# A hybrid decoder block on one core: input of the feed-forward part made earlier, weights prepared in pieces

## The chip, the cores and the metric

The kernel runs on 1 of the 8 cores of one Trainium2 chip. The metric is device time in microseconds (us) of one execution. TensorE (PE in the profile) multiplies matrices, VectorE (DVE), ScalarE (ACT) and GpSimd (POOL) work on elements, SyncE (SP) issues every DMA of this kernel in order.

## The reference

One decoder layer, `x` of 2048 tokens by 1024 channels, float32:

```
h = RMSNorm(x);  P = h @ W_in            # split among three mixers and three gates
ya, yb, yc = RG-LRU, mLSTM, stick-breaking attention (each projected to 1024)
x = x + (sigmoid(g_a)*ya + sigmoid(g_b)*yb + sigmoid(g_c)*yc) @ W_o
hf = RMSNorm(x);  gate, up = split(hf @ W_ffn_in)      # 2 x 2816 columns
x = x + (silu(gate)*up) @ W_ffn_out
out = RMSNorm(x)
```

## The kernel before

Tokens are worked in 4 chunks of 512 (c = 0 to 3), channels in tiles of 128 partitions. The stages follow each other: S (projections, LRU, mLSTM, attention), then `G` and `G_out` for each chunk, then F1 (feed-forward in), then F2 (feed-forward out and the last norm). The code is written with a tile library: a scheduler orders the instructions of each engine by the program's order as priority and by its own estimate of when an operand is there; tiles come from pools, and a tile waits until the memory it takes is free. What stands in an engine's queue then runs strictly in that order.

`G` computes the gates and merges the branches (tiles `pg`, `py`, `mh`, `ml`); `G_out` multiplies by W_o (`po`), adds x, writes x1 to `dX1` and sums its squares. At its end `rstd` makes the norm's factors: a product with ones (`pss`), a power on GpSimd (`nrs`), diagonals (`ndg`), a product that spreads them over the partitions (`psr`).

The feed-forward part uses Strassen-Winograd products: blocks of two by two, seven products instead of eight, each in three f16 products (high and low part). A weight block is loaded (`raw`), summed on GpSimd (`sm`, lines 826 to 829), scaled by an exponent (`squares` on ScalarE, `pse` on TensorE, `power` on VectorE) and split into `wh` (ScalarE) and `wl` (VectorE) by `wforms`. `F_input` does the same for the normed input of two chunks: four loads, four norms on VectorE (line 904), four sums on GpSimd (848 to 851), high parts on ScalarE (908), low parts on VectorE (909); it yields 4 tiles `f` (k = 0 to 3) of 7 forms. Chunks 0 and 1 form one side (cp = 0), chunks 2 and 3 the other (cp = 1).

F1 runs 22 weight blocks for each side, 84 products a block: 3696 products. `forms` splits the result of each pair of blocks and writes it to `dA`; F2 reads it back in three groups of pairs (0 to 3, 4 to 7, 8 to 10), 1848 products. `F2_scales` takes the largest exponent over all 11 pairs before the first weight of F2 can be scaled.

Of the kernel before, what the change touches and what calls it, by code (L numbers as in the profile page):

```python
# [18 lines left out]
P = 128  # L19
# [16 lines left out]
class Trunk:  # L36
# [10 lines left out]
    def setup(self):  # L47
# [20 lines left out]
        self.dR2 = dr.tile([NCH, P, CH], F32, name="dR2")  # L68
        self.dRow = dr.tile([NCH, 2, 4, CH], F32, name="dRow")
        self.dA = dr.tile([2, NPAIR, P, 7, 2, CH], F16, name="dA")  # L70
        self.dX2 = dr.tile([KT, 2, P, CH], F32, name="dX2")

# [4 lines left out]
    def constants(self):  # L77
        nc, cp = self.nc, self.cp

        def const(name, shape):  # L80
            t = cp.tile(shape, F32, name=name)
            nc.sync.dma_start(t, self.I[name])
            return t

        self.g2 = const("g_ffn", [P, KT])
        self.g3 = const("g_fin", [P, KT])
# [8 lines left out]
        for nm in ("wa", "wx"):  # L95
            for j in range(2):
                t = cp.tile([P, P], F32, name=f"bd{nm}{j}")
# [56 lines left out]
    HO = None  # L154

# [56 lines left out]
    def rstd(self, pool, acc, tag, bufs, ps="m", copy=True, sqrt=False, ps0=None):  # L212

        nc, V = self.nc, self.nc.vector
        ps0 = ps0 or ps
        pss = self.ps.tile([P, CH], F32, tag=ps0, name="pss", bufs=self.NP[ps0])
# [4 lines left out]
        rs = self.rs = pool.tile([P, NB], F32, tag="nrs", name="nrs", bufs=2)  # L221
        if sqrt:
            nc.scalar.activation(rs, pss[:, :NB], AF.Sqrt, scale=1.0 / 1024.0, bias=self.eps)
            V.reciprocal(rs, rs)
        else:
            V.tensor_scalar(rs, pss[:, :NB], 1.0 / 1024.0, 1e-6, op0=ALU.mult, op1=ALU.add)
            nc.gpsimd.tensor_tensor(rs, rs, self.nhalf, op=ALU.pow)
        dg = pool.tile([P, NB, P], F32, tag=tag, name="ndg", bufs=bufs)
        for b in range(NB):
            V.tensor_scalar(dg[:, b, :], self.idn, rs[:, b : b + 1], None, op0=ALU.mult)  # L230
        psr = self.ps.tile([P, CH], F32, tag=ps, name="psr", bufs=self.NP[ps])
        for b in range(NB):
            nc.tensor.matmul(psr[:, b * P : (b + 1) * P], self.ones, dg[:, b, :], start=True, stop=True)
        if not copy:
            return psr
        R = pool.tile([P, CH], F32, tag=tag, name="R", bufs=bufs)
        nc.scalar.activation(R, psr, AF.Copy)
        return R

# [463 lines left out]
    def G(self, c, hs):  # L703
# [10 lines left out]
        for j in range(KT):  # L714
# [19 lines left out]
            mer.append((mh, ml))  # L734
        return mer

    def G_out(self, c, mer):
# [17 lines left out]
        R = self.rstd(gp, acc, "m", 2)  # L755
        nc.sync.dma_start(self.dR2[c], R)


    def F_constants(self):
        nc, V, fr = self.nc, self.nc.vector, self.fr  # L760
        self.ones16 = fr.tile([P, P], BF, name="ones16")
        nc.gpsimd.memset(self.ones16, 1.0)

        def row(name, *values):
            t = fr.tile([P, len(values)], F32, name=name)
            for i, v in enumerate(values):
                nc.gpsimd.memset(t[:, i : i + 1], v)
            return t


        self.sgn = row("sgn", -1.0, -1.0, -1.0, -1.0, 1.0)
        self.off = row("off", 202.0, 52.0)

        ga = fr.tile([P, 1], BF, name="ga", bufs=1)
        self.squares(self.g2, ga)
        t = self.exponent(ga)
        sh = self.power(t, row("goff", 197.0))
        self.gs = fr.tile([P, KT], F32, name="gs", bufs=1)
        V.tensor_scalar(self.gs, self.g2, sh[:, 0:1], None, op0=ALU.mult)
        self.offh = fr.tile([P, 2], F32, name="offh", bufs=1)  # L780
        nc.gpsimd.memset(self.offh[:, 0:1], 202.0)
        V.tensor_scalar(self.offh[:, 1:2], t, 1.0, -18.0, op0=ALU.mult, op1=ALU.add)

    def squares(self, src, acc, junk=None):

        if junk is None:
            junk = self.fr.tile(list(src.shape), mybir.dt.uint8, tag="junk", name="junk", bufs=1)
        with self.nc.allow_low_precision(reason="only the exponent of the sum is used"):
            self.nc.scalar.activation(junk, src, AF.Square, accum_out=acc)

    def exponent(self, acc, a=""):

        nc, V = self.nc, self.nc.vector
        ps = self.ps.tile([P, CH], F32, tag="m", name="pse", bufs=1)
        nc.tensor.matmul(ps[:, 0:1], self.ones16, acc, start=True, stop=True)
        t = self.fr.tile([P, 1], I32, tag=a + "sce", name=a + "sce", bufs=2)
        V.tensor_scalar(t, ps[:, 0:1].bitcast(I32), 24, None, op0=ALU.logical_shift_right)
        return t

    def power(self, t, off, a=""):  # L800

        V, fr = self.nc.vector, self.fr
        n = off.shape[-1]
        e = fr.tile([P, 5], I32, tag=a + "scx", name=a + "scx", bufs=2)[:, :n]
        V.scalar_tensor_tensor(e, self.sgn[:, 5 - max(n, 2) :][:, :n], t, off, op0=ALU.mult, op1=ALU.add)
        f = fr.tile([P, 5], I32, tag=a + "scf", name=a + "scf", bufs=4)[:, :n]
        V.tensor_scalar(f, e, 23, None, op0=ALU.logical_shift_left)
        return f.bitcast(F32)

    def split2(self, hi, lo, x, s):  # L810
        self.nc.scalar.activation(hi, x, AF.Copy, scale=s)  # L811
        self.nc.vector.scalar_tensor_tensor(lo, x, s, hi, op0=ALU.mult, op1=ALU.subtract)  # L812

    def wforms(self, src, n, off):


        nc, fr, G = self.nc, self.fr, self.nc.gpsimd
        raw = fr.tile([P, 4, n], F32, tag="raw", name="raw", bufs=2)
        nc.sync.dma_start(raw, src)
        acc = fr.tile([P, 1], BF, tag="wacc", name="wacc", bufs=2)  # L820
        self.squares(raw, acc)
        f = self.power(self.exponent(acc), off)
        m = f.shape[-1] - 1
        sm = fr.tile([P, 3, n], F32, tag="sm", name="sm", bufs=1)
        a21, a11, a12, a22 = [raw[:, i] for i in range(4)]
        G.tensor_tensor(sm[:, 0], a21, a22, op=ALU.add)  # L826
        G.tensor_tensor(sm[:, 1], sm[:, 0], a11, op=ALU.subtract)
        G.tensor_tensor(sm[:, 2], a12, sm[:, 1], op=ALU.subtract)
        G.tensor_tensor(a21, a11, a21, op=ALU.subtract)
        wh = fr.tile([P, 7, n], F16, tag="wh", name="wh", bufs=2)  # L830
        wl = fr.tile([P, 7, n], F16, tag="wl", name="wl", bufs=2)
        if m == 1:
            for at, x in ((1, raw[:, 1:3]), (S1, sm[:, 0:2]), (0, raw[:, 0:1]), (A22, raw[:, 3:4]), (S4, sm[:, 2:3])):
                k = x.shape[1]
                self.split2(wh[:, at : at + k], wl[:, at : at + k], x, f[:, 0:1])
        else:
            for i in range(m):
                c = slice(i * P, (i + 1) * P)
                for at, x in ((0, raw), (4, sm)):
                    k = x.shape[1]  # L840
                    self.split2(wh[:, at : at + k, c], wl[:, at : at + k, c], x[:, :, c], f[:, i : i + 1])
        return (wh, wl), f[:, m : m + 1]

    def sums(self, q, tt):

        G = self.nc.gpsimd
        b12, b11, b21, b22 = [q[:, i] for i in range(4)]
        G.tensor_tensor(tt[:, 0], b12, b11, op=ALU.subtract)
        G.tensor_tensor(tt[:, 1], b22, tt[:, 0], op=ALU.subtract)
        G.tensor_tensor(tt[:, 2], b21, tt[:, 1], op=ALU.subtract)  # L850
        G.tensor_tensor(b12, b22, b12, op=ALU.subtract)
        return tt

    def slot(self, i):
        return (self.fl if i else self.fr).tile([P, 7, 2, CH], F16, tag="f", name="f", bufs=4)

    def product(self, ps, w, i, x, j, n, start):

        mm = self.nc.tensor.matmul
        wh, wl = w  # L860
        for k in range(n):
            ks = slice(k * P, (k + 1) * P)
            f = x[k]
            mm(ps, wh[:, i, ks], f[:, j, 0], start=start and k == 0, stop=False, skip_group_check=True)  # L864
            mm(ps, wh[:, i, ks], f[:, j, 1], start=False, stop=False, skip_group_check=True)  # L865
            mm(ps, wl[:, i, ks], f[:, j, 0], start=False, stop=k == n - 1, skip_group_check=True)  # L866


    STEPS = [("p", A11, B11), ("q", S1, T1), ("p", S2, T2), ("r", A12, B21), ("p", S3, T3), ("q", S4, B22), ("p", A22, T4)]
    PSF = dict(p="d", q="z", r="s")  # L870

# [354 lines left out]
```

## Time and profile before

| | |
|---|---|
| median of 3 runs (lowest, highest) | 3023.54 us (3021.39, 3025.41) |
| profiled execution, its span | 3026.73 us, 3025.0 us |
| busy: PE, DVE, ACT, POOL | 2838.8, 1962.6, 1318.9, 728.1 us |
| mean granted TensorE clock | 0.963 of 2.4 GHz |
| moved by DMA | 398.85 MB |

The stages in that execution: S to about 1175 us (attention of the last chunk reaches into G), G and G_out to 1655, F1 to 2544, F2 to 3025. A share of busy time is a mean over stages; what the end hangs on is read stage by stage. Waits are put down to the signal that came last.

### The profile page before, as it was taken

The page shows a single profiled execution, that of the slowest core. Times are in us where ns is not written, and L with a number is a line of the kernel's source. Part 1 is how long each engine was busy: PE and PEld are TensorE (multiplying, and loading weights), DVE is VectorE, ACT ScalarE, POOL GpSimd, SP SyncE. Part 2 cuts the span into 40 slices and gives each one's busy share as a digit, 9 for nine tenths or more (in the row PEclk, how much of TensorE's full clock was granted, in tenths as well). Part 3 has the DMA queues.
Part 4 walks back from the last instruction along what each step waited for, and adds up shares of the span by engine and source line. Part 5 has one row for each costly group of instructions (what it writes and reads, how often), then busy time and mean ns, then how long its engine had stood idle before and what let it go on. Part 6 is the DMA issues. An engine that isn't in the chain of part 4 may idle for free.

```text
span 3025.0 us, 36457 instructions
## 1 busy us (share of the span) xinstructions
PE 2838.8 (94%) x13405; PEld 1870.1 (62%) x13405; DVE 1962.6 (65%) x2793; ACT 1318.9 (44%) x1975; POOL 728.1 (24%) x876
## 2 busy tenths in 40 slices
PE   8999999999999999999998479999999996899996
PEld 7777878777877887888887134444444442344443
DVE  7677888987777765345343875555555554657667
ACT  4445464644554543223222444444444452434432
POOL 0022323322232210000000653233233231323221
PEclk9999999999999999999999699999999998899998
DMA  5454545354355325335324211222222226336433
GB/s 174 149 175 144 185 139 166 118 168 169 108 169 171 105 91 188 115 97 194 100 94 169 78 66 66 77 77 84 77 84 85 79 77 250 143 146 257 181 116 143
DMA packets 153171, 398.85 MB, mean 132 GB/s; under 512 B 18176, under 2 KB 38656, under 8 KB 144800
## 3 DMA queue, kind: packets, MB, share of 16 engines
q1 hardware_dynamic: 152992, 396.53, 38.0%
q8 instruction: 105, 1.72, 0.2%
q14 instruction: 74, 0.61, 0.1%
HBM read 307.79 MB, written 88.67 MB: 131 GB/s over the span
## 4 chain that ended last, share of the span: by engine, by line
PE 81%; DVE 8%; DMA 5%; issue 3%; ACT 2%; POOL 1%; SPq 0%; DVEq 0%; ACTq 0%; POOLq 0%
PE pfp L864 7%; PE pfp L866 7%; PE pfp L865 7%; PE pg L197 6%; PE pg L195 6%; PE pg L196 6%; PE pfq L864 3%; PE pfq L866 3%; PE pfq L865 3%; PE psd L195 3%; PE psd L197 3%; PE psd L196 3%; PE pt L689 2%; PE pfr L864 2%; PE pfr L865 2%
## 5 line engine op out<-in xcount | busy, mean ns | idle before, releaser
L176 DVE TENSOR_TENSOR wl<-wraw,wh 128x768 fp32r<-128x768 f32 (+2 forms) x232 | 285.1, 1230 | 282.7 <-ACT wh L168 281.9
L168 ACT ACTIVATE wh<-wraw 128x768 fp32r<-128x768 f32 (+2 forms) x232 | 238.6, 1030 | 462.0 <-PE pg L196 202.3
L864 PE MATMUL pfp<-f,wh 128*128 128x512 f16 x1056 | 403.4, 383 | 35.7 <-ACT f L908 22.4
L865 PE MATMUL pfp<-f,wh 128*128 128x512 f16 x1056 | 404.1, 383 | 8.3 <-DVE f L909 8.3
L866 PE MATMUL pfp<-f,wl 128*128 128x512 f16 x1056 | 401.0, 383 | 0.0
L864 PEld LDWEIGHTS <-wh 128*128 128x128 f16 x1848 | 182.3, 99 | 266.4 <-issue 34.3
L866 PEld LDWEIGHTS <-wl 128*128 128x128 f16 x1848 | 181.8, 98 | 235.7 <-issue 15.7
L865 PEld LDWEIGHTS <-wh 128*128 128x128 f16 x1848 | 182.1, 99 | 231.6 <-issue 24.1
L197 PE MATMUL pg<-hh,wl 128*128 128x512 f32 x768 | 305.5, 398 | 2.8 <-DVE wl L176 2.8
L195 PE MATMUL pg<-hh,wh 128*128 128x512 f32 x768 | 305.8, 399 | 1.2 <-ACT sgg L725 0.7
L196 PE MATMUL pg<-hl,wh 128*128 128x512 f32 x768 | 303.1, 395 | 1.6 <-POOL hl L176 1.6
L864 PE MATMUL pfq<-f,wh 128*128 128x512 f16 x528 | 201.7, 382 | 13.2 <-ACT wh L811 9.4
L866 PE MATMUL pfq<-f,wl 128*128 128x512 f16 x528 | 200.9, 382 | 4.1 <-DVE wl L812 4.1
L865 PE MATMUL pfq<-f,wh 128*128 128x512 f16 x528 | 201.9, 382 | 0.6 <-DVE f L909 0.6
L195 PE MATMUL psd<-hh,wh 128*128 128x512 f32 x448 | 183.9, 411 | 2.8 <-DVE scl L315 2.8
L826 POOL TENSOR_TENSOR sm<-raw 128x512 f32<-128x512 f32 (+1 forms) x46 | 66.1, 1436 | 496.8 <-DVE wl L812 380.1
L197 PE MATMUL psd<-hh,wl 128*128 128x512 f32 x448 | 180.8, 403 | 0.5 <-DVE wl L176 0.5
L196 PE MATMUL psd<-hl,wh 128*128 128x512 f32 x448 | 180.0, 402 | 0.0
L811 ACT ACTIVATE wh<-raw,scf 128x512 f16<-128x512 f32 (+1 forms) x154 | 116.1, 771 | 126.1 <-PE pfp L865 52.4
L197 PEld LDWEIGHTS pg<-hh,wl 128*128 128x128 f32 x768 | 145.8, 190 | 39.2 <-DVE wl L176 5.2
L196 PEld LDWEIGHTS pg<-hl,wh 128*128 128x128 f32 x768 | 144.7, 188 | 35.8 <-POOL hl L176 2.0
L195 PEld LDWEIGHTS pg<-hh,wh 128*128 128x128 f32 x768 | 144.6, 188 | 33.2 <-ACT sgg L725 0.9
(301 smaller groups left out, 6105.2 us busy)
## 6 DMA issues: line engine op xcount, KB each, us to landing
wraw<-in_wG SPq DMA_DIRECT2D x96, 512.0 KB, 3.5
f<-dA SPq DMA_DIRECT2D x22, 1792.0 KB, 14.5
wraw<-in_wS SPq DMA_DIRECT2D x56, 512.0 KB, 3.6
x<-in_xT SPq DMA_DIRECT2D x88, 256.0 KB, 4.0
raw<-in_wF SPq DMA_DIRECT2D x22, 1024.0 KB, 4.8
dA<-fs SPq DMA_DIRECT2D x44, 512.0 KB, 2.6
dA<-fs SPq DMA_DIRECT2D x22, 768.0 KB, 3.4
wraw<-in_wO SPq DMA_DIRECT2D x32, 512.0 KB, 5.3
```

The lines of the kernel that those rows point to most:

```text
L168: nc.scalar.activation(dst, src, AF.Copy)
L176: (self.nc.gpsimd if pool else self.nc.vector).tensor_tensor(lo, src, hi.bitcast(F32), op=ALU.subtract)
L195: nc.tensor.matmul(ps, wh, hh, start=start and i == 0, stop=False)
L196: nc.tensor.matmul(ps, wh, hl, start=False, stop=False)
L197: nc.tensor.matmul(ps, wl, hh, start=False, stop=stop and i == n - 1)
L689: PE.transpose(pt[:, i * P : (i + 1) * P], As[i][:, js], self.idn)
L811: self.nc.scalar.activation(hi, x, AF.Copy, scale=s)
L826: G.tensor_tensor(sm[:, 0], a21, a22, op=ALU.add)
L864: mm(ps, wh[:, i, ks], f[:, j, 0], start=start and k == 0, stop=False, skip_group_check=True)
L865: mm(ps, wh[:, i, ks], f[:, j, 1], start=False, stop=False, skip_group_check=True)
L866: mm(ps, wl[:, i, ks], f[:, j, 0], start=False, stop=k == n - 1, skip_group_check=True)
```

## The change

1. The norm factors of each chunk stay in SBUF as one column (`rs2`), and are spread when they are used.
2. The input of side 0 is made by a generator, `input_first`, that `G` and `G_out` of chunks 2 and 3 step on, after each of their eight rounds, in memory (`fa`) that attention leaves. Weights of F1 are formed from `G_out` of chunk 3 on.
3. The input of side 1, `input_second`, is stepped on between the products of F1. F1 therefore runs weight blocks 0 to 3 for side 0 alone, then the same four for side 1, with the weights loaded and split a second time.
4. `wforms` and `forms` are generators too, stepped after each product of twelve; forms are split and written in pieces of 512 columns instead of up to 1536.
5. F2 scales each group of pairs by its own largest exponent (`scales`); x1 is loaded one quarter ahead. The last two weight blocks of F1 run side 0 first, both blocks, then side 1.
6. All pools wait tile by tile for the memory they take over; small constants move.

```diff
+    def rstd_columns(self, pool, acc, ps0, sqrt=False, rs=None):
...
     def put_y(self, pool, i, c, y):
         th = pool.tile([P, CH], FR, tag="yh", name="yh", bufs=1)
-        tl = pool.tile([P, CH], FR, tag="yl", name="yl", bufs=1)
+        tl = y.bitcast(FR)
...
+    def wforms(self, src, n, off):
+        raw = wk.tile([P, 4, n], F32, tag="raw", name="raw", bufs=2)
+        nc.sync.dma_start(raw, src)
+        yield
...
+        G.tensor_tensor(a21, a11, a21, op=ALU.subtract)
+        yield
+        yield
+        f = self.power(self.exponent(acc), off() if callable(off) else off)
+        yield
+...
+    def advance(self):
+        if self.at in self.work and not self.hold:
+            self.work[self.at].step()
+...
+    def seven(self, q, t, put):
+        b12, b11, b21, b22 = [q[:, i] for i in range(4)]
+        G.tensor_tensor(t, b12, b11, op=ALU.subtract)
+        put(B11, b11)
+        yield
+        put(T1, t)
+        G.tensor_tensor(t, b22, t, op=ALU.subtract)
+        yield
+        put(B21, b21)
+        yield
+        put(T2, t)
+        G.tensor_tensor(t, b21, t, op=ALU.subtract)
...
+    def parts(self, f, q, t):
+        yield from self.seven(q, t, lambda i, x: self.split2(f[:, i, 0], f[:, i, 1], x,
+            eng=self.nc.gpsimd if i in (B11, B21, B22) else None))
...
+    def input_second(self, out, quad, tt, pool):
+        q = self.x1_load(1, 0, quad())
+        dg = [self.diagonals(pool, r, "fs", 3) for r in self.rs2[2:4]]
+        R = [self.spread(d, "s") for d in dg]
+        for k in range(KT // 2):
+            for u, j in self.PLACE:
+                self.normed(k, q, u, j, self.gs2, R)
...
+            yield from self.parts(f, q0, tt())
...
-    def G(self, c, hs):
+    def G(self, c, hs, steps=0):
...
+            for _ in range(steps):
+                self.advance()
...
-        R = self.rstd(gp, acc, "m", 2)
-        nc.sync.dma_start(self.dR2[c], R)
+            for _ in range(steps):
+                self.advance()
+        self.rstd_columns(gp, acc, "m", rs=self.rs2[c])
...
+        for cp in range(2):
+            for b in range(4):
+                self.blocks([side(cp, b % 2, *self.next_weights())], 4)
+                if b % 2:
+                    forms(b // 2, cp)
+            if cp == 0:
+                xf1.finish()
...
+        ws = [self.next_weights(), self.next_weights()]
+        self.hold = True
         for cp in range(2):
             for up in range(2):
                 self.blocks([side(cp, up, *ws[up])], 4)
+                self.hold = cp == 0
+            last = forms(NPAIR - 1, cp)
...
+                if opens and gi == 0 and q == 1:
+                    fc = opens()
+                if len(xs) == q + 1 < 4 and (fc or q == 0):
+                    x_load()
...
                 for c in range(NCH):
-                    mer = self.G(c, hs)
+                    mer = self.G(c, hs, (0, 0, 3, 3)[c])
...
-                    self.G_out(c, mer)
+                    self.G_out(c, mer, 3 if c == NCH - 1 else 0)
```

TensorE's queue around the end of `G_out` of chunk 3, before: all products `po` stand ahead of the norm, and the first product of F1 (`pfp`) comes after both.

```order
L196 MATMUL po<-ml,wh 128x512
L197 MATMUL po<-mh,wl 128x512
L218 MATMUL pss<-ones,xacc 128x1 x4
L233 MATMUL psr<-ndg,ones 128x128 x4
L795 MATMUL pse<-ga,ones_15150 128x1
L795 MATMUL pse<-wacc,ones_15150 128x1
L864 LDWEIGHTS wh
L864 MATMUL pfp<-f,wh 128x512
```

The same place now (`pfp`, `pfq` are products of the first block of F1): 12 products of F1 stand in the middle of the 192 products `po`, ten more a little later.

```order
L202 MATMUL po<-mh,wl 128x512
L875 LDWEIGHTS wh
L875 MATMUL pfp<-f,wh 128x512
L876 MATMUL pfp<-f,wh 128x512
L877 MATMUL pfp<-f,wl 128x512
...
L875 MATMUL pfq<-f,wh 128x512
L200 MATMUL po<-mh,wh 128x512
...
L877 MATMUL pfr<-f,wl 128x512
L231 MATMUL pss<-ones,xacc 128x1 x4
L764 MATMUL pse<-wacc,ones_379 128x1
L255 MATMUL psr<-ndg,ones 128x128 x2
```

So 22 of the first block's 84 products moved ahead of the norm of chunk 3.

GpSimd's queue after the same point, before (`tt`, `xq`: sums of the input of either side; `sm`, `raw`: sums of a weight block).

```order
L227 TENSOR_TENSOR nrs<-nrs,nhalf 128x4
L848 TENSOR_TENSOR tt<-xq 128x512
L849 TENSOR_TENSOR tt<-xq,tt 128x512
L851 TENSOR_TENSOR xq<-xq 128x512
L850 TENSOR_TENSOR tt<-xq,tt 128x512
```

And now, from the power of chunk 3's norm on (`hq`, `ht`: input of side 1; `f<-hq,f`: a low part, which VectorE made before).

```order
L241 TENSOR_TENSOR rs_88<-rs_88,nhalf 128x4
L782 TENSOR_TENSOR f<-hq,f 128x512 x2
L919 TENSOR_TENSOR ht<-hq 128x512
L802 TENSOR_TENSOR sm<-raw 128x512
L782 TENSOR_TENSOR f<-hq,f 128x512
L933 TENSOR_TENSOR hq<-hq 128x512
L803 TENSOR_TENSOR sm<-sm,raw 128x512
L923 TENSOR_TENSOR ht<-hq,ht 128x512
L804 TENSOR_TENSOR sm<-raw,sm 128x512
L928 TENSOR_TENSOR ht<-hq,ht 128x512
L805 TENSOR_TENSOR raw<-raw 128x512
```

Three low parts of each input tile came to GpSimd, and the sums of side 1 now alternate with those of weights.

SyncE's queue where F1 ends, before (`dA<-fs`: forms out; `f<-dA`: forms of four pairs in; `xf`: x1 in).

```order
L958 DMA dA<-fs 128x3072
L1042 DMA f<-dA 128x7168 x5
L958 DMA dA<-fs 128x2048
L1042 DMA f<-dA 128x7168 x3
L958 DMA dA<-fs 128x2048
L1007 DMA xf<-dX_81 128x512 x4
```

And now.

```order
L1024 DMA dA<-fs 128x1024 x12
L1197 DMA f<-dA 128x7168 x3
L1024 DMA dA<-fs 128x1024
L1197 DMA f<-dA 128x7168
...
L793 DMA raw<-in_wP 128x2048
L1197 DMA f<-dA 128x7168 x3
L1024 DMA dA<-fs 128x1024
L1197 DMA f<-dA 128x7168
L1024 DMA dA<-fs 128x1024 x2
L793 DMA raw<-in_wP 128x2048
L1024 DMA dA<-fs 128x1024 x3
L1169 DMA xf<-dX_81 128x512 x4
```

The four loads for the first group now stand well ahead, between the forms of pair 9; the four of the second group stand ahead of all forms of pair 10, and x1 behind them.

## Rows read from the trace of the kernel before

**Rows 1.** The page, the span in 40 equal slices, busy tenths.

```profile
PE   8999999999999999999998479999999996899996
```

**Rows 2.** Busy time by stretch: stretch, length, PE, PEld, DVE, ACT, POOL, clock, DMA share, GB/s.

```profile
1230.00:1656.00 426.00, 421.49 (x1820) 341.50 (x1820) 176.17 (x219) 126.71 (x169) 7.15 (x15) 1.00 0.38 127
1656.00:1823.00 167.00, 102.31 (x386) 42.32 (x387) 135.02 (x137) 68.56 (x77) 89.68 (x55) 0.75 0.22 76
1823.00:2544.00 721.00, 720.22 (x3370) 326.73 (x3368) 417.37 (x568) 336.84 (x426) 227.62 (x155) 1.00 0.22 83
2544.00:2584.00 40.00, 1.14 (x7) 0.41 (x4) 6.65 (x23) 6.34 (x6) 5.05 (x4) 0.57 0.78 322
...
2560.00:2570.00 10.00, 0.00 (x0) 0.00 (x0) 0.37 (x1) 0.00 (x0) 0.00 (x0) 0.50 1.00 425
...
2950.00:3025.00 75.00, 50.05 (x224) 26.81 (x222) 53.75 (x94) 20.17 (x33) 7.78 (x8) 0.83 0.40 143
```

**Rows 3.** Timeline of PE: start, us, instruction; three places.

```profile
1654.30 0.40 PE L197 MATMUL po<-mh,wl 128*128 128x512 f32 x1
...
2000.08 0.38 PE L864 MATMUL pfq<-f,wh 128*128 128x512 f16 x1
2000.29 0.38 PE L865 MATMUL pfq<-f,wh 128*128 128x512 f16 x1
2000.51 0.38 PE L866 MATMUL pfp<-f,wl 128*128 128x512 f16 x1
...
2544.27 0.38 PE L866 MATMUL pfp<-f,wl 128*128 128x512 f16 x1
...
2584.20 0.61 PE L864 MATMUL pfp<-f,wh 128*128 128x512 f16 x1 [1.84 <-ACT wh L811]
```

**Rows 4.** Waits of PE, 1650 to 2600 us: in total, times, longest.

```profile
PE pse L795 <- ACT fs L789: 39.5, 3, 36.1
PE pfp L864 <- ACT f L908: 22.4, 5, 8.9
```

**Rows 5.** The chain that ended last, in order of time: start, us, what.

```profile
1663.83 9.32 DVE xq L904 x8
...
1680.74 5.76 DVE xq L904 x4
...
2543.15 14.67 DMA dA<-fs
...
2560.40 11.47 DMA dA<-fs
```

**Rows 6.** Timeline of POOL and of DVE at 1680 and 1707 us.

```profile
1684.23 1.71 POOL L851 TENSOR_TENSOR xq<-xq 128x512 f32<-128x512 f32 x1
1685.90 1.71 POOL L850 TENSOR_TENSOR tt<-xq,tt 128x512 f32<-128x512 f32 x1
...
1707.86 1.26 POOL L849 TENSOR_TENSOR tt<-xq,tt 128x512 f32<-128x512 f32 x1
...
1680.74 5.75 DVE L904 SCALAR_TENSOR_TENSOR xq<-xq,gs,Rf 128x512 f32<-128x512 f32 x4
```

**Rows 7.** Groups by shape, 1815 to 2540 us: count, busy us, mean ns, idle before.

```profile
L929 DVE SCALAR_TENSOR_TENSOR aq<-cm,scf,aq 128x512 f32<-128x512 f32 x119 | 109.6, 933 | 24.9 <-ACT aq L928 22.9
...
L812 DVE SCALAR_TENSOR_TENSOR wl<-raw,scf,wh 128x512 f16<-128x512 f32 x40 | 33.4, 857 | 0.4 <-ACT wh L811 0.4
...
L812 DVE SCALAR_TENSOR_TENSOR wl<-raw,scf,wh 128x1024 f16<-128x1024 f32 x20 | 28.6, 1432 | 10.3 <-ACT wh L811 10.3
...
L937 DVE TENSOR_TENSOR cm<-pfp,cm 128x512 f32<-128x512 f32 x39 | 26.9, 691 | 69.4 <-PE pfp L866 62.1 <-PE pse L795 6.9
L812 DVE SCALAR_TENSOR_TENSOR wl<-sm,scf,wh 128x1024 f16<-128x1024 f32 x20 | 26.3, 1315 | 0.1
...
L812 DVE SCALAR_TENSOR_TENSOR wl<-sm,scf,wh 128x512 f16<-128x512 f32 x20 | 14.9, 744 | 0.2 <-ACT wh L811 0.2
...
L805 DVE SCALAR_TENSOR_TENSOR scx<-sgn,sce,offh 128x2 int32<-128x2 f32 x18 | 9.0, 499 | 0.3
```

**Rows 8.** DMA issues by line: count, KB each, median us to landing.

```profile
xf<-dX SPq DMA_DIRECT2D x32, 256.0 KB, 4.4
```

More of the change, by code (lines that the diff above doesn't have):

```diff
@@ L71, in setup @@
         self.dX2 = dr.tile([KT, 2, P, CH], F32, name="dX2")
+        self.rs2 = [cp.tile([P, NB], F32, name=f"rs2{c}") for c in range(NCH)]
     def first_constants(self):
@@ new lines, in squares, with exponent @@
+    def squares(self, src, acc, junk):
+        with self.nc.allow_low_precision(reason="only the exponent of the sum is used"):
+            self.nc.scalar.activation(junk, src, AF.Square, accum_out=acc)
+    def exponent(self, acc, a=""):
+        nc, V = self.nc, self.nc.vector
+        n = acc.shape[-1]
+        ps = self.psum(self.map["e"], "pse")
+        for i in range(n):
+            nc.tensor.matmul(ps[:, 0:1], self.ones16, acc[:, i : i + 1], start=i == 0, stop=i == n - 1)
+        t = self.cp.tile([P, 1], I32, tag=a + "sce", name=a + "sce", bufs=2)
+        V.tensor_scalar(t, ps[:, 0:1].bitcast(I32), 24, None, op0=ALU.logical_shift_right)
+        return t
@@ new lines, in advance, with finish @@
+    def advance(self):
+        if self.at in self.work and not self.hold:
+            self.work[self.at].step()
+        self.fills = [f for f in self.fills if not f[0].done]
+        first = True
+        for f in self.fills:
+            if f[1] is None:
+                if first:
+                    f[0].step()
+                first = False
+                continue
+            f[2] += f[1]
+            while f[2] >= 1.0:
+                f[2] -= 1.0
+                f[0].step()
+    def finish(self, *ws):
+        for w in ws:
+            w.finish()
@@ new lines, with blocks @@
+    PSF = dict(p="d", q="z", r="s", e="m")
+    PSI = dict(p="d", q="z", r="av", e="m")
+    map = PSF
+    DONE = {3: (0, 0), 4: (1, 1), 5: (1, 0), 6: (0, 1)}
+    def blocks(self, sides, n, order=None):
+        pss = [{} for _ in sides]
+        if order is None:
+            order = [(0, 0), (0, 1), (1, 0), (1, 1), (2, 0), (2, 1), (3, 0), (4, 0), (4, 1), (5, 0), (6, 0), (3, 1), (6, 1), (5, 1)]
+            if len(sides) == 1:
+                order = [(i, 0) for i in range(7)]
+        for o in order:
+            if callable(o):
+                o()
+                self.advance()
+                continue
+            step, u = o
+            w, x, then = sides[u]
+            acc, i, j = self.STEPS[step]
+            new = acc not in pss[u]
+            if new:
+                pss[u][acc] = self.psum(self.map[acc], "pf" + acc)
+            ps = pss[u][acc]
+            self.product(ps, w, i, x, j, n, new)
+            then(step, ps)
+            self.advance()
@@ L784, in squares @@
[L784 to L842, printed above, removed]
@@ L857, in product @@
[L857 to L869, printed above, removed]
@@ L870 @@
-    PSF = dict(p="d", q="z", r="s")
-    def blocks(self, sides, n):
-        pss = [{} for _ in sides]
-        order = [(0, 0), (0, 1), (1, 0), (1, 1), (2, 0), (2, 1), (3, 0), (4, 0), (4, 1), (5, 0), (6, 0), (3, 1), (6, 1), (5, 1)]
-        if len(sides) == 1:
-            order = [(i, 0) for i in range(7)]
-        for step, u in order:
-            w, x, then = sides[u]
-            acc, i, j = self.STEPS[step]
-            new = acc not in pss[u]
-            if new:
-                tag = self.PSF[acc]
-                pss[u][acc] = self.ps.tile([P, CH], F32, tag=tag, name="pf" + acc, bufs=self.NP[tag])
-            ps = pss[u][acc]
-            self.product(ps, w, i, x, j, n, new)
-            then(step, ps)
@@ L1034, in then @@
                 norm(u, j, q)
-        nxt = prep(0)
         for gi, (p0, n) in enumerate(FGROUPS):
```

448 lines of the change are left out of this document (303 added, 145 removed).

## Prediction

> **What bounds the kernel now.** I read the page's slices first [rows 1]: TensorE is full nearly everywhere, with dips in the slices at about 1660 to 1810 us, near 2550 us and at the end. The table of stretches [rows 2] puts sizes on them. In G and G_out of the last chunks (1230 to 1656 us) PE is busy 421.5 of 426 us, in F1's steady part 720.2 of 721. Between them, from 1656 to 1823 us, it is busy 102 of 167 us at a granted clock of 0.75, and from 2544 to 2584 us not at all to speak of. VectorE, 41% busy in G and 58% in steady F1, is 81% busy in the first gap (135.0 of 167).
>
> *Gap one.* The last product of G_out ends at 1654.7 us and F1's last at about 2544.5 [rows 3]: 889.8 us for 3696 products. In steady F1 they follow each other in 0.2155 us [rows 3], so at that pace they take 796.5. Lost: 93.3 us. The chain [rows 5] says to what: norms of the two sides' input on VectorE, and PE's waits [rows 4] name the high parts `f` (22.4 us). All of the input of side 0 stands between G_out and the first product.
>
> *Gap two.* From 2544.5 to 2584.2 us PE waits 39.7 us, 36.1 of them in one wait for the exponent of F2's scales [rows 4]; with 1.4 for products at half clock behind it, 41 us. The chain shows two writes of `dA` of 14.7 and 11.5 us [rows 5], which queue with the loads `f` of four pairs, at 425 GB/s [rows 2].
>
> The third dip, the last 75 us [rows 2], the change doesn't touch.
>
> The profiled execution took 3026.73 us (span 3025.0, 1.7 outside it), 3.2 above the median of 3023.54. I work in it and take 3.2 off at the end.
>
> **Gap one after the change.** The input of side 0 now lies under G and G_out of chunks 2 and 3. Side 1 must still wait for chunk 3's norm, and its input is made while F1 runs four weight blocks for side 0. So the question is whether it is ready when PE comes to side 1.
>
> When PE gets there: the first product that reads the form T1 of side 1's fourth tile is F1's 390th. 22 of the 389 ahead of it are already done within G_out, so 367 x 0.2155 = 79 us, and about 3 us for the norm's own small products: 82 us after G_out's end.
>
> When the input is ready has three answers.
> - GpSimd by itself: that form's sum is its 44th operation after the norm's power (sums of the input, 12 low parts new to it, sums of weights). One takes 1.26 us alone and 1.71 beside VectorE [rows 6]: 55 to 75 us, and with a start about 9 us after G_out, 64 to 84. It works in order, so a low part that waits for a norm holds the sums of the next weight behind it; two weights ready ahead cover that.
> - VectorE by itself: 5 weights' splits, each 2 x 0.857 + 1.432 + 1.315 + 0.744 = 5.2 [rows 7], are 26.0; their 6 scales, some 0.75 with a small one beside (0.499 is the row), 4.5; 16 `aq` at 0.933, 14.9; 13 adds at 0.691, 9.0; 16 norms; 13 low parts, like `wl` of 512 at about 0.9, 11.7; small ones about 8. A norm now reads its factor from PSUM, which no row shows: not under the 0.69 of an add that reads PSUM, not over the 1.44 of a norm before [rows 6, 7]. I take 0.75, near the add, which has the same operands: 12. The sum is 86, the form ready at 88 us (at 1.44 each, 99).
> - The two together. While VectorE makes norms, GpSimd's sums start 1.67 us apart and take 1.71 instead of 1.26, and the norms take 1.44, twice an add of the same size [rows 6, 7]. One sum and about one norm came out of each 1.67 us, so the two worked rather one after the other than side by side: with 0.69 of it for VectorE, about 1.0 is GpSimd's. If that holds for every VectorE operation with two operands in SBUF, the splits, low parts and `aq` (26.0 + 11.7 + 14.9 = 52.6) and 44 x 1.0 = 44 of GpSimd add up: 97 us, and some 3 to start, 100.
>
> I take the third, since the rows show it: PE waits 100 - 82 = 18 us for side 1. With 4 for the norm's small products and the clock after them, and 4 for evacuations that come late in blocks 5 to 8 behind a full VectorE, 26 us of the 93 remain: **-67**. Bounds: 11 remain when the engines don't hold each other (form at 88), 45 when norms stay at 1.44 under the same hold (form at about 119).
>
> The Trainium skill, "SBUF — State Buffer", section "Who interferes with whom", speaks against this change here: a VectorE instruction with two SBUF inputs contends with a GpSimd instruction that reads SBUF, by a read interface that they share and that the page calls an exclusive lock. The change moves low parts to GpSimd beside a VectorE that is full. By that rule the loss is the 26 us above, without it about 12; the trace agrees as far as it goes (1.71 against 1.26 us).
>
> **G and G_out of chunks 2 and 3** take what left the gap: on VectorE 16 norms, the low parts and diagonals of side 0 that are not GpSimd's, some 24 operations of 0.75 to 1.44 us, 20 to 35 us in 426 us where it is 41% busy; on GpSimd sums and low parts, where it is busy 7 us. PE has nothing to wait for there but PSUM: +3 (0 to 12). On SyncE the loads of x1 for this (`fq`) now stand among the loads of gate weights, and a load that waits for its memory holds the weights behind it. Weights ahead cover it: two raw and two ready, each the work of some 5.6 us, about 22 us. A tile's chain (four norms, four sums, low parts) is about 20, so I count none.
>
> At nothing: the mixers' low part made in place, the earlier constants, the finer waits for memory (PE is full in all of S but the slices of rows 1), and four more weights loaded, 4 MB where the DMAs are 22% busy [rows 2]. Without that cover, 4 MB at 425 GB/s would be 10 us. Forms split in pieces of 512 give more, smaller operations on VectorE, in 42% idle time. The program's start may shift by 2 either way.
>
> **Gap two after the change.** F2's first group of scales no longer needs the last pair, so PE has work when F1 ends: 36 products of quarter 0 and 36 of quarter 1, but what it makes must leave PSUM, and this takes x1. On SyncE the four loads of the second group (7.3 MB) stand ahead of the forms of pair 10 and x1 stands behind these. Their memory comes free only when F1 is done (T'). 7.3 MB at 425 GB/s are 17 us; the forms go out in seven pieces over three buffers, the first at T' + 14.7 as the chain had it [rows 5], the next two near + 19, the next three + 21 to 23; then x1 takes 4.4 [rows 8]: the first result leaves PSUM at about T' + 27. PE's work till then is 36 x 0.2155 = 7.8: idle 19, half clock after it 2, and about 3 for x1 of quarter 1. 24 of 41 remain: **-17**. Bounds: 12 when the writes go out between the loads, 41 when nothing is gained.
>
> **Sum.** -67 - 17 + 3 = -81: 3026.7 - 81 = 2945.7 for a profiled execution, 2942 as a median.
>
> **Rivals.**
> - *Nearly all idle time goes.* VectorE and GpSimd don't hold each other, and x1 is there in time. For it: the count of each engine by itself gives 64 to 88 us against 82. Against: rows 6, and SyncE's order of loads. 12 us and 5 us remain of the gaps: -(93 - 12) - (41 - 5) = -117, 2907. Chance 0.13.
> - *VectorE is the bound of the first eight one-sided blocks.* These are 8 x 84 x 0.2155 = 145 us. VectorE has 417/721 of their time, 84 us, four extra weights at about 6 (24), 16 norms at 1.44 (23), 16 low parts (15) and about 20 of small pieces: 166. In the gap before, it got no further than 81% [rows 2]: 166/0.81 = 205, so 60 are lost, and 4 as above; gap two stays as it was. -(93 - 64) + 3 = -26: 2997. For it: VectorE is the engine that the gap hung on. Against: norms from PSUM should be shorter, and 12 low parts went to GpSimd. Chance 0.15.
> - *Slower than before.* SyncE stands still in G of chunk 2 with a load of x1 that waits for GpSimd to be done with the tile before, weights of the gates behind it. Two such waits (tiles 1 and 2) cost PE what they exceed 22 us. They eat the gain of 84 when each is over 22 + 42 = 64 us; at 70 each the time is 3023.5 - 84 + 96 = 3036. Against: a tile's chain of 20 us would have to be three times as long, beside a GpSimd that has nothing else to do. Chance 0.04.
> - *It doesn't do what it says.* The 12 products of F1 in the middle of G_out wait there for weights or forms, and TensorE loses in G_out what it saved. Before, the first weights of F1 were split in the gap; now SyncE loads them among W_o. Result within 0.2%. Chance 0.02.
>
> **How the numbers follow.** The forecast has 0.66: 2942, its own range 2905 to 2975 by the bounds (11 to 45, 12 to 41 and 0 to 12, not all at one end). The range of 8 in 10 takes in the first rival below and half of the second above: 2890 to 2998. About 0.2%, 6 us, is what a measurement of this kernel can tell from no change. Faster: 0.66 + 0.13 + 0.15 = 0.94; within it 0.02; slower 0.04.
>
> **What would show it.** After G_out's end PE runs at full clock through side 0's four blocks, then stops once for some 18 us about 82 us later, waiting for a low part or T1 of side 1, with VectorE and GpSimd both near full and GpSimd's operations nearer 1.7 than 1.26 us. If PE instead waits in many short stops over blocks 5 to 8, VectorE is the bound (second rival). A norm that reads PSUM is under 0.9 us. At F1's end PE stops about 19 us for VectorE's sum with x1, which waits for the DMA `xf`, and not for `fs`. G and G_out of chunks 2 and 3 are together within 12 us of what they were. I am wrong if gap one keeps more than 45 us, or if PE waits for weights in G.

## The result, and the profile after

The changed kernel took 2951.11 us (median of 4 runs, 2948.06 to 2956.11) against 3024.23 before: ratio 0.9761, 95% interval 0.9744 to 0.9778, 73 us less. Forecast were 2942 and -81. The profiled execution has a span of 2949.5 us, 75.5 less than before.

The page's slices, PE's busy tenths, answer to [rows 1]: the dip behind slice 21 is shallow now, the one at F1's end shorter.

```profile
PE   8999999998999999999999989999999999799996
```

Busy time by stretch, columns as in [rows 2]: G and G_out of chunks 2 and 3, the first 145 us behind G_out, steady F1, F1's end with F2's start, and the program's end.

```profile
1230.00:1657.00 427.00, 419.90 (x1800) 336.73 (x1799) 220.55 (x247) 144.25 (x197) 66.37 (x40) 0.99 0.40 130
1657.00:1802.00 145.00, 123.31 (x551) 54.97 (x550) 117.96 (x156) 85.11 (x122) 87.85 (x61) 0.94 0.28 98
1802.00:2489.00 687.00, 686.88 (x3218) 311.58 (x3217) 423.38 (x643) 343.23 (x493) 218.00 (x154) 1.00 0.24 90
2489.00:2540.00 51.00, 29.99 (x123) 12.51 (x122) 28.39 (x47) 19.63 (x28) 16.81 (x13) 0.83 0.83 311
2875.00:2949.50 74.50, 51.77 (x231) 26.05 (x228) 56.80 (x100) 21.76 (x35) 7.91 (x8) 0.85 0.41 144
```

Where gap one lost 65 us of PE in 167, it now loses 22 in 145, at a clock of 0.94 instead of 0.75. VectorE is as busy as before (118 of 145, 81%). G has taken 44 us of VectorE and 59 of GpSimd, and PE is still busy 420 of 427 us.

PE's waits from 1645 to 1830 us answer to [rows 4]: in total, times, longest.

```profile
PE pfp L875 <- ACT wh L784: 7.6, 2, 3.9
PE pfp L875 <- DVE cm L1126: 6.2, 3, 3.9
PE pse L764 <- ACT wl L756: 3.1, 1, 3.1
PE pfp L876 <- DVE f L782: 2.3, 1, 2.3
PE pfq L876 <- DVE f L782: 1.2, 1, 1.2
```

`wh` and `pse` are weights (10.7 us), `cm` is a result that leaves PSUM late (6.2), `f` the input of side 1 (4.3 with two waits under 1 us).

Around F1's end, PE's waits from 2480 to 2560 us:

```profile
PE pse L764 <- ACT fj L756: 12.5, 1, 12.5
PE pfp L875 <- ACT wh L784: 3.9, 1, 3.9
PE pfp L875 <- DVE xf L1188: 3.5, 2, 2.2
PE pfq L875 <- DVE xf L1188: 1.0, 1, 1.0
```

The chain of the same stretch, its writes of forms: start, us, what.

```profile
2491.83 14.78 DMA dA<-fs
...
2508.22 7.74 DMA dA<-fs
...
2519.40 4.84 DMA dA<-fs
```

21 us of stops stand where 40 stood. The first write of `dA` still takes 14.8 us, as in [rows 5].

To weigh kernels by stage I count products. Lost in gap one: the time from G_out's last product to F1's last, less 0.2155 us [rows 3] for each product between them. "From F1's end": from there to the end of the span, with products of F2 that ran before F1's end (36 in most kernels) put at the same 0.2155. This is needed because the start of G_out of chunk 1, up to which these kernels run nearly the same work, lies anywhere between 1161 and 1172 us in their profiles.

| kernel | lost in gap one | from F1's end | from G_out's end to the end |
|---|---|---|---|
| before | 93.5 | 480.3 | 1370.3 |
| changed | 36.2 | 464.7 | 1292.4 |
| low_vector | 45.0 | 464.3 | 1300.8 |
| low_gpsimd | 43.5 | 467.7 | 1302.8 |
| no_norm | 42.5 | 462.1 | 1296.1 |
| side1_out | 9.9 | 459.6 | 1261.0 |
| few_weights | 14.4 | 466.3 | 1272.2 |
| side0_late | 98.5 | 463.7 | 1358.7 |
| one_scale | 35.5 | 460.8 | 1287.8 |
| forms_first | 36.3 | 459.6 | 1287.5 |
| sides_together | 36.4 | 473.0 | 1301.0 |
| six_blocks | 39.3 | 459.3 | 1290.1 |
| rate | 38.8 | 462.4 | 1292.7 |
| gp_queue | 34.7 | 468.5 | 1298.4 |

So the 75.5 us are 57.3 from gap one, 15.6 from F1's end, and 2.6 from what lies before G_out's end (it ends 2.4 later, with 23 products, 5.0 us, of F1 in it).

How well a stretch repeats can be read from kernels that share it. The changed kernel, one_scale, forms_first and sides_together have the same gap one: 35.5 to 36.4. The changed kernel, low_vector, low_gpsimd, no_norm and few_weights have the same end of F1: 462.1 to 467.7. So 6 us more lost in gap one is a difference, and 3 us at F1's end is none. Each row is one execution.

### The profile page after: what moved, and what is told of

It is laid out like the page before. It is cut to its first block, busy times and chain, and to the rows that moved or that the text cites. A ratio compares the mean times of both kernels' runs of the same rounds, so it can differ in the third digit from the quotient of the medians.

```text
span 2949.5 us, 37052 instructions
## 1 busy us (share of the span) xinstructions
PE 2827.9 (96%) x13409; PEld 1866.0 (63%) x13409; DVE 1994.5 (68%) x2933; ACT 1362.6 (46%) x2122; POOL 782.2 (27%) x916
## 4 chain that ended last, share of the span: by engine, by line
PE 80%; DVE 8%; DMA 4%; issue 3%; ACT 2%; POOL 2%; SPq 0%; DVEq 0%; POOLq 0%; ACTq 0%
PE pfp L875 7%; PE pfp L876 7%; PE pfp L877 7%; PE pg L202 5%; PE pg L201 5%; PE pg L200 5%; PE pfq L875 3%; PE pfq L876 3%; PE pfq L877 3%; PE psd L200 3%; PE psd L202 3%; PE psd L201 3%; PE pt L707 2%; PE pfr L875 2%; PE pfr L876 2%
## 5 line engine op out<-in xcount | busy, mean ns | idle before, releaser
L784 ACT ACTIVATE wh<-raw,scf 128x512 f16<-128x512 f32 (+1 forms) x166 | 127.1, 781 | 113.9 <-DVE scf L776 104.5
L200 PEld LDWEIGHTS pg<-hh,wh 128*128 128x128 f32 x768 | 146.3, 191 | 36.4 <-ACT wh L173 3.9
```

Of the source, the lines that this page charges most:

```text
L200: nc.tensor.matmul(ps, wh, hh, start=start and i == 0, stop=False)
```

## The experiments

Ratios are to the kernel before, run on the same chip; the changed kernel's is 0.9761 (0.9744 to 0.9778).

**side0_late**: side 0's norms wait for chunk 3's (`late` makes `rs2b` from 0 times chunk 3's factors plus their own), and `G` and `G_out` step nothing.

```diff
-                self.nc.vector.tensor_scalar(dg[:, b, :], self.idn, self.rs2[u][:, b : b + 1], None, op0=ALU.mult)
+                self.nc.vector.tensor_scalar(dg[:, b, :], self.idn, self.rs2b[u][:, b : b + 1], None, op0=ALU.mult)
...
-                    mer = self.G(c, hs, (0, 0, 3, 3)[c])
+                    mer = self.G(c, hs)
...
-                    self.G_out(c, mer, 3 if c == NCH - 1 else 0)
-                    if c == 1:
+                    self.G_out(c, mer)
+                    if c == NCH - 1:
+                        self.late()
```

> The input of side 0 is made after chunk 3's norm instead of under G and G_out (its norm factors are made to depend on chunk 3's); the rest as changed. Theory (what lies under G is the gain of gap one): four tiles one after the other, about 20 us each, stand ahead of side 0's blocks, 50 to 80 us longer, 3001 to 3031, and G of chunk 2 loses its two stops. Rival (pieces of weights and one side at a time would hide it beside products as well): 10 to 25 longer.

3002.21 us, ratio 0.9919 (0.9892 to 0.9947). 98.5 us are lost in gap one again, 62 more, first of all in waits for side 0's forms (`pfr` on ScalarE's and GpSimd's parts of `f`):

```profile
PE pfr L875 <- ACT f L781: 12.2, 3, 6.1
PE pfr L876 <- POOL f L782: 10.4, 1, 10.4
```

G of chunk 2 has no stop for weights and takes 167.9 us. Without what lies under G and G_out, all of gap one's gain is gone. The sums of F1's second weight block come after G_out here too, but PE's stops for weights hardly change (11.4 us against 10.7).

**low_vector** and **low_gpsimd**: the low parts of side 1.

```diff
# low_vector: no low part on GpSimd
-            yield from self.parts(f, q0, tt())
+            yield from self.parts(f, q0, tt(), False)
...
# low_gpsimd
-            yield from self.parts(f, q0, tt())
+            yield from self.parts(f, q0, tt(), (B11, B21, B22, T3, T4))
```

> The 12 low parts of side 1 that the change gave to GpSimd are made on VectorE again. Theory A (the two engines shut each other out, so the sum of both counts; a low part costs GpSimd about 1.0 us of the shared time and VectorE about 0.7): gap one, which loses 40 us in the changed kernel, gets about 4 shorter, 2947, or stays. Rival B (VectorE by itself is the bound of that stretch): 12 x 0.7 to 1.3 = 8 to 16 longer, 2959 to 2967.

2962.67 us, 0.9784 (0.9769 to 0.9798): 8.8 us more lost in gap one. Theory A falls, B fits so far.

> Eight more low parts of side 1 (of T3 and T4) go from VectorE to GpSimd. Theory B (VectorE by itself bounds F1's first blocks): VectorE has 8 x 0.7 to 1.2 = 6 to 10 us less to do, and the way from G_out's end to the program's end (1292.4 us in the changed kernel's profile) gets 5 to 9 shorter; time about 2945. Theory A (the sum of both engines counts): 8 x (1.0 - 0.7), 2 to 4 us longer, 2954. Rival C (GpSimd becomes the bound: 8 x 1.46 = 12 more on its 92 of 153 us): longer by 5 or more.

2959.50 us, 0.9780 (0.9758 to 0.9801): 7.3 us more lost in gap one. B said less, A a little more; the size is that of rival C, but GpSimd is busy for only 94.0 of the first 145 us here, so its time alone is not the bound. More work on either engine costs, and less on VectorE gives nothing: A and B are both too simple.

**no_norm**: the 16 norms of side 1 left out.

```diff
-            for u, j in self.PLACE:
-                self.normed(k, q, u, j, self.gs2, R)
```

> The 16 norms of side 1 are left out (its input goes on unscaled): VectorE has 16 x 0.739 = 11.8 us less in gap one, GpSimd and ScalarE the same. Theory B (VectorE is the bound): 8 to 12 us shorter from G_out's end to the end, 1281 to 1284. Rival (what counts is the latency of preparing weights: load, exponent, GpSimd's sums): within 3 us of 1292.

2959.86 us, 0.9775 (0.9753 to 0.9797), 6.3 us more lost with 11.8 us of work less; from G_out's end to the end it is 3.7 us more. The whole time can't be told from the changed kernel's, but it is not 8 to 12 us shorter: B has fallen. Both results, this one and low_gpsimd's, missed what I expected. Why leaving work out lengthens the gap is not settled; side 1's operations come to the other queues earlier (its last low part starts 106 us after G_out's end instead of 117), and PE no longer waits for side 1 but longer for `cm` (12.7 us).

```profile
PE pfp L875 <- ACT cm L1121: 6.4, 4, 1.8
PE pfp L875 <- DVE cm L1124: 6.3, 3, 3.1
```

**side1_out** and **few_weights**: what competes in gap one, one of the two left out, one run each.

```diff
# side1_out
-                f = self.fill(self.input_second(
+                xf[1] = xf[0]
+                f = self.fill(iter(()) if True else self.input_second(
...
# few_weights: blocks 0 and 1 are used for all eight
-                self.blocks([side(cp, b % 2, *self.next_weights())], 4)
+                self.blocks([side(cp, b % 2, *two[b % 2])], 4)
...
-        for b in [0, 1, 2, 3, 0, 1, 2, 3] + list(range(4, 2 * NPAIR)):
+        for b in [0, 1] + list(range(4, 2 * NPAIR)):
```

> Left out: the whole input of side 1 (side 1 is computed with side 0's input), so VectorE has 28 operations and GpSimd 28 fewer in gap one; the eight one-sided blocks with their eight weights stay. PE stops 21.7 us in gap one of the changed kernel, 10.7 of it for weights, 6.2 for results that leave PSUM late, 4.3 for side 1. Theory W (one-sided blocks use each weight once, and preparing one takes as long as two blocks, whatever else runs): the stops for weights stay, over 8 us. Theory D (it is the two together: weights and evacuations wait only because side 1's input stands among them in the same queues): all stops together fall under 5 us, and F1's end comes 25 to 33 us nearer to G_out's end (836.3 us to the last sum of F1).

2912.72 us (VectorE has 32 operations fewer, not 28 as I wrote). Stops 3.1 us for weights and next to nothing else; lost 9.9 us, 26.3 less. Theory D, not W. The first 145 us behind G_out:

```profile
1650.00:1795.00 145.00, 141.17 (x663) 63.35 (x661) 109.11 (x148) 84.06 (x117) 57.55 (x41) 1.00 0.26 91
```

VectorE is still 75% busy here and ScalarE as busy as in the changed kernel, and PE runs full: the one-sided blocks by themselves fit.

> Left out: six of the eight preparations of weights in the one-sided blocks (blocks 0 and 1 are used for all); side 1's input stays. Theory W: stops for weights go, those for side 1 stay at 4 or grow to 10, since PE comes to it earlier. Theory S (side 1's chain through one buffer, four tiles one after the other, is slow by itself): side 1 is ready at 115 us after G_out's end as now, and PE waits there for 20 us or more in one place. Theory D: side 1's input is ready 20 us or more earlier, at 95 us or before, and all stops up to there are under 8 us; a stop of up to 10 us for the weights of the first two-sided block comes after.

2929.12 us, 14.4 lost. Side 1's last low part on VectorE starts at 1738.9 us, 84 us after G_out's end instead of 117; no wait for side 1, 7.7 us for `cm`. D again; S falls, and so does W, which had PE still waiting for side 1.

What is left of gap one, then, comes from the two together, and VectorE's time alone is not its bound (no_norm). What D may look like in a queue is seen on ScalarE of the changed kernel, 1657 to 1802 us:

```profile
ACT f L781 <- DVE hq L940: 11.3, 8, 3.0
ACT aq L1117 <- DVE cm L1126: 10.4, 7, 3.1
ACT wh L784 <- DVE scf L776: 6.8, 4, 2.8
ACT f L781 <- POOL hq L933: 5.2, 2, 2.7
```

ScalarE, 59% busy, stands still over 16 us with a high part of side 1 at its head that waits for a norm or a sum, with weights and evacuations in order behind it. Each input tile goes back and forth between VectorE, GpSimd and ScalarE, and each step waits behind others' work. Standing still is no loss by itself: in few_weights ScalarE waits over 30 us with such high parts at its head (25 here, all of them counted), and PE stops for 8. It costs where something that PE needs next stands behind. That this is the cause of the remaining stops is a reading of the queues; no run changed the order alone and got the time back.

**six_blocks** and **rate** tried to make room (both with forms_first's edit).

```diff
# six_blocks
-            for b in range(4):
+            for b in range(6):
...
-        for b in [0, 1, 2, 3, 0, 1, 2, 3] + list(range(4, 2 * NPAIR)):
+        for b in 2 * list(range(6)) + list(range(6, 2 * NPAIR)):
...
# six_blocks and rate
-                ), 1.3)
+                ), 0.9)
```

> Six weight blocks instead of four run one side at a time (two more weights loaded twice), the fill's rate goes from 1.3 to 0.9 so that it spreads over them, and the loads of F2's second group stand behind the forms as in forms_first. Theory D (weights and evacuations wait because side 1's input stands among them): the same input stands among 1.5 times the blocks, the stops of gap one fall from 21.7 to about 12 us and F1's last sum comes 8 to 12 us nearer to G_out's end (826); with the second edit the time is about 2934. Rival (each more one-sided block brings its own preparation of a weight and so no room): 836 or later, time 2944 as forms_first.

2950.64 us, 0.9745 (0.9730 to 0.9760); 39.3 lost. The rival held: waits for side 1 are gone, those for `cm` grew to 13.8 us, and all stops together are 21 in the first 175 us, as before. forms_first, the kernel to compare with, has 0.9723 and 36.3.

> Order alone: four one-sided blocks as in the changed kernel, but the fill's rate is 0.9 instead of 1.3, so that weights stand ahead of the last tile of side 1 in the queues; the work is the same; loads behind forms as in forms_first. If the order decides: stops for weights fall from 10.7 to under 6 us, and stops for side 1 grow by 5 or more, since its last tile comes later; F1's last sum moves by 4 us or more from 836.4, either way. If only the amount of work decides: 836 within 2 us.

2950.58 us, 0.9742 (0.9722 to 0.9762); 38.8 lost, 2.5 more than forms_first. Stops for weights are 7.4, for side 1 6.3: traded, as the order would have it, but less than expected, and with no gain.

**gp_queue**: the stops in G.

```diff
-            self.nc.sync.dma_start(q[:, at], self.dX1[2 * cp + u, k + 4 * j])
+            (self.nc.sync if cp else self.nc.gpsimd).dma_start(q[:, at], self.dX1[2 * cp + u, k + 4 * j])
```

> The 16 loads of x1 for the input of side 0 are issued by GpSimd instead of SyncE, so that a load which waits for its memory holds no weights behind it. Theory (SyncE held weights of the gates in G of chunk 2, where PE stops twice, 5.5 us, and then runs at half clock, some 9 us lost): these stops go, 2942. Rival (the split of those weights is late because VectorE is full of norms there): stops stay, within 3 us of 2951.

2959.85 us, 0.9778 (0.9763 to 0.9793): no gain, PE's stops in G of chunk 2 are 6.4 us instead of 5.5. So SyncE alone was not the cause. In the changed kernel these stops are:

```profile
PE pg L200 <- ACT wh L173: 2.9, 1, 2.9
PE pg L202 <- DVE wl L181: 2.6, 1, 2.6
```

The timeline of its ScalarE shows another candidate:

```profile
1254.63 1.18 ACT L781 ACTIVATE f<-fq 128x512 f16<-128x512 f32 x2 [2.30 <-POOL fq L928]
1259.75 1.18 ACT L781 ACTIVATE f<-fq 128x512 f16<-128x512 f32 x2 [3.94 <-POOL fq L919]
1260.83 1.04 ACT L173 ACTIVATE wh<-wraw 128x1024 fp32r<-128x1024 f32 x1
```

ScalarE idles 3.9 us for a sum of GpSimd, with a high part at the head of its queue; the high part `wh` of the gate's weights, for which PE stops at 1259 us, stands behind it. In gp_queue it waits there 3.2 and 1.2 us, and the stop stays. No run took the high part out of this place; side0_late, without side 0's input in G, has no such stop.

**sides_together**, **one_scale**, **forms_first**: F1's end.

```diff
# sides_together: last two weight blocks as the others
-        for b in range(4, 2 * NPAIR - 2):
+        for b in range(4, 2 * NPAIR):
...
# one_scale
-        V.tensor_reduce(tm, tf, axis=mybir.AxisListType.X, op=ALU.max)
+        V.tensor_reduce(tm, tg, axis=mybir.AxisListType.X, op=ALU.max)
...
-            for p in range(p0, p0 + n):
+            for p in range(NPAIR):
...
# forms_first: ahead of each load of F2's second group
+                if cp == 0 and gi == 1:
+                    nc.scalar.activation(f[:, 0, 0, 0:2], self.last_fs[:, 0, 0:2], AF.Copy)
```

> The last two weight blocks of F1 run both sides together again, so all forms of pair 10 and all eight first loads of F2 come at F1's end; scales by group stay. Theory (the order of the last blocks is what brought the 20 us of gap two: it lets the first group's loads and side 0's forms begin 36 us before F1's end): gap two is back at 35 to 45 us, 1292 + 15 to 22 from G_out's end, time about 2969. Rival (forms in pieces and x1 a quarter ahead brought it): within 5 us.

2958.72 us, 0.9777 (0.9757 to 0.9798). From F1's end 8.3 us more; the stop for `pse` is 23.9 instead of 12.5:

```profile
PE pse L764 <- ACT fj L756: 23.9, 1, 23.9
```

The order of the last blocks is worth about half of the 15.6 us, less than expected.

> F2's scales are taken from the largest exponent over all 11 pairs again, as in the kernel before; all else as changed. Theory (the group's own scale is what lets F2 begin): F2's first weights wait for the last pair's exponent again, and the 72 products (15.5 us) that now lie ahead of the stop fall behind it: 2951 + 15 to 20, about 2968. Rival (the stop is set by the loads and x1 alone, scales are a side matter): within 5 us of 2951.

2946.79 us, 0.9732 (0.9717 to 0.9747): rather faster than the changed kernel, where I expected 17 us more. The theory falls, and the rival, within 5 us of 2951, held. SyncE's order is that of the changed kernel but for one load: all eight loads of F2's first two groups stand ahead of pair 10's forms, and x1 stands behind the first six writes of these.

```profile
2445.50 1.38 SPq L1199 DMA_DIRECT2D f<-dA  x3
...
2448.17 0.47 SPq L1199 DMA_DIRECT2D f<-dA  x1
...
2476.27 2.26 SPq L1199 DMA_DIRECT2D f<-dA  x4
2478.63 2.87 SPq L1024 DMA_DIRECT2D dA<-fs  x3
2486.80 8.54 SPq L793 DMA_DIRECT2D raw<-in_wP  x2
2499.25 3.75 SPq L1024 DMA_DIRECT2D dA<-fs  x3
2508.20 1.74 SPq L1171 DMA_DIRECT2D xf<-dX  x4
```

What I expected to fall behind the stop did not: 72 products of F2 run ahead of it here as in the changed kernel, after a wait for the common scale.

```profile
PE pse L764 <- DVE tm L1036: 2.3, 1, 2.3
```

F2 starts with side 0 and needs the scales of side 0 alone, and side 0's pair 10 is through two blocks before F1's end. With the last blocks in this order, then, a scale for each group gains nothing that this run can show.

> The four loads of F2's second group wait until the last form of pair 10 is made, so on SyncE they stand behind all writes of forms (two tiny copies make that order). Theory (the 12.5 us stop for the exponent comes from writes of forms queued behind 7.3 MB of loads, which keep the three form buffers occupied): that stop falls under 4 us, 2951 - 8 to 14, about 2940. Rival (the exponent is late because of its own chain on ScalarE, VectorE and GpSimd): no more than 3 us change. Second rival: group two then comes late and PE stops there for 5 us or more.

2943.98 us, 0.9723 (0.9707 to 0.9740), the best version that was run. The one write of forms in its chain from 2485 to 2545 us:

```profile
2491.81 2.04 DMA dA<-fs
```

PE's waits in it from 2480 to 2560 us:

```profile
PE pfp L875 <- ACT wh L784: 6.2, 1, 6.2
PE pse L764 <- ACT wl L756: 4.2, 2, 2.1
PE pfp L875 <- DVE xf L1189: 2.8, 3, 1.7
PE pfq L875 <- ACT wh L784: 2.1, 1, 2.1
```

The 12.5 us stop is gone and the write takes 2.0 us instead of 14.8: the writes were late because of the second group's loads ahead of them (7.3 MB, of which three loads of four stand ahead of the first write). No product waits for these loads, so the second rival falls too. 5.1 us less from F1's end, not much more than kernels with the same end differ by; F2's first weight (6.2) takes part of the place. The ratio's 11 us is more than this stretch shows; the rest I can't place.

## Why the prediction was right, step by step

- **Gap one**, forecast 26 lost (-67), measured 36.2 (-57). The mechanism, side 0's input hidden under G and G_out, is shown by side0_late. The inside of the sum was wrong. "PE waits 100 - 82 = 18 us for side 1" was 4.3; "4 for evacuations that come late" was 6.2, and 10.7 went to weights, which I had covered by "two weights ready ahead". The stops together, 21.5, are near the 22 forecast by accident of these errors. PE came to the 390th product not 82 but 104.8 us after G_out's end, put back by 16.6 us of stops and by products at half clock, and so it waited there for 0.5 us only:

```profile
1762.33 0.38 PE L875 MATMUL pfq<-f,wh 128*128 128x512 f16 x1 [0.51 <-ACT f L781]
```

  The form itself (T1 of the fourth tile) was ready at 109.0 us with its low part, and not at 100. Behind three of the stops 31 products ran at half clock, 6.6 us; the norm's small products took 4.0. As the prediction's own test had it, many short stops point to the second rival; but VectorE's time as such wasn't the bound (no_norm). Work in order on several engines is what the queues show in its place; it is not shown by a run of its own. GpSimd's sums and low parts took 1.49 us on the average, half way between 1.26 and 1.71. The lower bound of 11 has a slip (88 - 82 + 4 + 4 is 14), and the bounds all at one end give 2912 and not 2905; neither touches the result.
- **The hold of the two engines** changes durations, but adding up does not give the time. Groups by shape, 1657 to 1802 us:

```profile
L1118 DVE SCALAR_TENSOR_TENSOR aq<-cm,scf,aq 128x512 f32<-128x512 f32 x18 | 21.8, 1212 | 1.9 <-ACT aq L1117 1.8
...
L782 DVE TENSOR_TENSOR f<-ht,f 128x512 f16<-128x512 f32 x12 | 14.1, 1174 | 5.4 <-ACT f L781 5.0
...
L940 DVE SCALAR_TENSOR_TENSOR hq<-hq,gs,psr 128x512 f32<-128x512 f32 x16 | 11.6, 739 | 2.0 <-DMA hq<-dX 2.0
...
L1118 DVE SCALAR_TENSOR_TENSOR aq<-pfp,scf,aq 128x512 f32<-128x512 f32 x6 | 4.5, 744 | 1.2 <-ACT aq L1117 1.2
```

  And in low_vector, 1660 to 1805 us, with 12 operations fewer on GpSimd:

```profile
L1118 DVE SCALAR_TENSOR_TENSOR aq<-cm,scf,aq 128x512 f32<-128x512 f32 x18 | 17.3, 961 | 0.9 <-ACT aq L1117 0.8
...
L785 DVE SCALAR_TENSOR_TENSOR fs<-aq,ascf,fs 128x512 f16<-128x512 f32 x8 | 10.4, 1298 | 0.0
```

  A norm that reads PSUM takes 0.739 us, as taken (0.75). `aq<-cm` takes 1.21 where it took 0.93 [rows 7]; the same operation on a result in PSUM (`aq<-pfp`) takes 0.744 in the same stretch. This agrees with the Trainium skill, "SBUF — State Buffer", section "Who interferes with whom": it is VectorE's instructions with two inputs in SBUF that get longer beside GpSimd. But which of them it hits moves: in low_vector `aq<-cm` is back at 0.96, and `fs<-aq` takes 1.30 instead of 0.96. Adding up what the two engines take, as I did from [rows 6], forecast the wrong sign for low_vector.
- **G and G_out**, forecast +3 (0 to 12). G of chunk 2 took 9.6 us more (from one G_out's end to the next one's start, 178.5 against 168.9 us): two stops, 5.5 us, and half clock; VectorE got 44 us of work there, not 20 to 35. "I am wrong if [...] PE waits for weights in G": it does, so here the prediction failed by its own test; by the timeline the weights stood behind ScalarE's high parts, which no run shows alone. From G_out of chunk 1 to G_out of chunk 3, end to end, it is 10.5 us more, 5.5 without the 23 products of F1, within the 12 allowed. A gain that I had not seen paid for it, which was luck: G_out of chunk 1 takes 47.0 us instead of 52.7. Before, PE waited there 4.2 us for `xr`, and now it doesn't; such waits in G_out of chunk 3 went from 2.9 to 1.1. In the kernel before, norms of the next chunk's input stood ahead of this addition on VectorE and waited for loads of `x`.
- **Gap two**, forecast 24 left (-17), measured -15.6. Its queue was read right in the main (the first write took 14.8 us, 14.7 was forecast; three and not four of the second group's loads stand ahead of it), and forms_first shows that it set the stop. The sign was wrong: not 19 us for VectorE's sum with x1 but 12.5 for `pse`, the exponent of side 1's last forms, and 4.5 for `xf`. And "F2's first group of scales no longer needs the last pair, so PE has work" is not what gained: with one scale for all pairs the same 72 products run ahead of the stop (one_scale). The order of the last blocks gave about half, and the rest wasn't taken apart.
- **The rivals.** Nearly all idle time goes: no, 36 and 21 us stay. Slower by a held SyncE: three loads of x1 did take SyncE 10.4 us in G of chunk 2 (from 1254.6 us), within the cover of 22, and in gp_queue PE's stop stays without them. It does what it says: 22 products of F1 start ahead of G_out's last one, a 23rd before it ends, and wait there for nothing over 0.3 us (36 run ahead of the norm, where I had put 22).

## What to carry to other kernels

When work moves beside a full engine, don't add up durations alone: look in each in-order queue at what stands at its head waiting for a third engine, and at what the bottleneck needs that stands behind it. Look at loads and writes of one DMA queue in the same way: four tiny copies that put 7.3 MB of loads behind the writes took away a stop of 12.5 us, where a scale for each group showed no gain. Compare stretches, since the time of a whole kernel also moves with what an edit does not touch, and before a result is explained, read in the experiment's own queue whether the order is what the edit was meant to make it.

## What the runs showed that I had not expected

- Two stops of the same length had different effects on TensorE's clock. Behind the stop of 3.87 us that ends at 1693.2 us, products follow each other in 0.2155 us (granted clock 1.00, 2.4 GHz). PE then works for 2.8 us and stops again for 3.93; behind this one they follow in 0.43 us (0.50, 1.2 GHz), until 1704.9 us. The timeline of PE in the changed kernel there:

```profile
1693.21 0.38 PE L875 MATMUL pfp<-f,wh 128*128 128x512 f16 x1 [3.87 <-DVE cm L1126]
1693.42 0.38 PE L876 MATMUL pfp<-f,wh 128*128 128x512 f16 x1
...
1699.89 0.61 PE L875 MATMUL pfp<-f,wh 128*128 128x512 f16 x1 [3.93 <-ACT wh L784]
1700.29 0.63 PE L876 MATMUL pfp<-f,wh 128*128 128x512 f16 x1
1700.71 0.63 PE L875 MATMUL pfr<-f,wh 128*128 128x512 f16 x1
```

- Leaving out 11.8 us of VectorE work from a stretch in which VectorE was 81% busy made it 6.3 us longer in the profiled execution.
